# Weighted values of attention for two query tiles at a time, in one row on TensorE

## The chip, the cores and the metric

The kernel runs on one core of a Trainium2 chip. The metric is the device time of one execution in microseconds; of several executions the median is taken.

## What is computed

One layer of an encoder trunk on 1024 positions of width 1024: a SwiGLU feed-forward block, then a mixing block of which one half is attention (8 heads of width 64) and the other a two-directional RWKV-7 scan, then a second feed-forward block, each between RMS norms and added to the residual stream. The change is in the attention:

```python
DILATED_PATTERNS = ((128, 1), (512, 4), (2048, 16))
for window, dilation in DILATED_PATTERNS:
    o, l = _dilated_attention(q, k, v, window, dilation)   # query i sees i + dilation*j, |j| <= window/(2*dilation)
    outs.append(o); lses.append(l)
wts = jax.nn.softmax(jnp.stack(lses, axis=0), axis=0)
o = jnp.sum(wts[..., None] * jnp.stack(outs, axis=0), axis=0)
```

with softmax weights `p = exp(s - m)` within each pattern and values `p @ v / sum(p)`.

## The kernel before

The kernel is written in stages: first feed-forward block (to about 680 us), projections, attention (some 910 to 1180 us), the scan (to about 1530 us), the second feed-forward block. Its author's code states what each step does and in which order it is wanted; a scheduler then places the instructions on each engine's queue, by the order of the code and by what it takes to be ready. An engine works through its queue in that order and waits where data or a buffer are missing. So code that is moved by one step can shift instructions of other steps too.

**Attention.** The first two patterns are handled together in `near` (L694), the third in `far` (L648); `attention` (L766) runs the heads one after the other and lets the far part of the next head run between the steps of the present one. Beside each head but the last, `beside(h)` issues a projection of the RWKV half (`project_rwkv`, L505, tile `zr`, L523): 48 matmuls of 128x512 that depend on nothing in the head, and that the scheduler uses as filling.

`near` works on 8 tiles of 128 queries. A tile sees the keys of up to five blocks of 128: 3, 4, 5, 5, 5, 5, 4 and 3 of them. For each tile t:

- `scores(t)`, L705: queries against keys on TensorE into PSUM (tile `s`, L713 and L714, in two halves of up to 512 and 128 columns; the inputs are in fp32r), then the bias and the row minimum on VectorE (L715, tile `nm`), then the exponential on ScalarE (L718, tile `sb`, with the row sum).
- `turn(t)`, L720: 3 to 5 transposes of 128x128 on TensorE into PSUM (tile `pt`, L727), copied to SBUF by ScalarE or VectorE (L728, tile `e12`; the profile calls it `e`). The pool of this tile has two buffers.
- `values(t)`, L730: for each key block two products, one for each half of the queries, into the PSUM tile `po` (L734, against `vn`). The two halves go to different column halves of TensorE's array (`c` = 0 and 64), so the two products of a block run side by side there. A product of fp32 data shows as two records in the profile; a tile with five key blocks has 10 products and 20 records.

The steps are staggered: `scores(step)`, `turn(step - 1)`, `values(step - 2)`, so that values are asked for in each of the steps 2 to 9, one tile at a time. After the last step VectorE scales `po` (L758, tile `ya`); `po` has one buffer, so the next head's first value product waits for L758.

In `far`, 16 products of 64x65 (L673) go into two PSUM tiles, `po3s` and `po3t`, in turns; one reads the upper half of the array's rows and the other the lower.

Of the kernel before, what the change touches and what calls it, by code (L numbers as in the profile page):

```python
# [10 lines left out]
F32 = mybir.dt.float32  # L11
# [20 lines left out]
def _ap(src, off, pat):  # L32
    return bass.AP(tensor=src.tensor, offset=src.offset + off, ap=pat)
# [130 lines left out]
class _Kernel:  # L164
# [138 lines left out]
    def product(self, psum, x, hl, which):  # L303

        return self.product_into([psum.tile([128, 512], F32, name="gu", tag="gu") for _ in which], x,
                                 [(h[:, k, :], l[:, k, :]) for h, l in hl for k in range(4)], which)
# [387 lines left out]
    def near(self, psum, p, h, sq, kh, kl, v, far, between):  # L694

        nc, V, A, G, T = self.nc, self.nc.vector, self.nc.scalar, self.nc.gpsimd, self.nc.tensor
        hs = slice(h % 2 * 64, h % 2 * 64 + 64)
        nm, d = (p.tile([128, NT], F32, name=n, tag=n) for n in ("nm", "dn"))
        M = p.tile([128, 4 * NT], F32, name="M", tag="M")[:, :NT]
        cc = p.tile([128, 2, NT], F32, name="cc", tag="cc")  # L700
        po = psum.tile([128, NT, 64], F32, name="po", tag="o", bufs=1)
        S_, E_ = {}, {}
        keys = lambda t: (max(0, t - 2), min(NT, t + 3))

        def scores(t):  # L705
            k0, k1 = keys(t)
            n, qs = (k1 - k0) * 128, slice(t * 128, (t + 1) * 128)
            bias = self.bias12[:, (k0 - t + 2) * 128:(k0 - t + 2) * 128 + n]
            s = S_[t] = p.tile([128, 640], F32, name="sb", tag="sb")
            for c in range(0, n, 512):  # L710
                e = min(n, c + 512)
                ps = psum.tile([128, 512], F32, name="s12", tag="s", bufs=2)
                T.matmul(ps[:, :e - c], sq[:, qs], kh[:, k0 * 128 + c:k0 * 128 + e], start=True, stop=False)  # L713
                T.matmul(ps[:, :e - c], sq[:, qs], kl[:, k0 * 128 + c:k0 * 128 + e], start=False, stop=True)  # L714
                V.tensor_tensor_reduce(out=s[:, c:e], in0=ps[:, :e - c], in1=bias[:, c:e], scale=-1.0,  # L715
                                       scalar=nm[:, t:t + 1] if c else 3e38, op0=OP.add, op1=OP.min,
                                       accum_out=nm[:, t:t + 1])
            A.activation(s[:, :n], s[:, :n], AF.Exp, bias=nm[:, t:t + 1], scale=-1.0, accum_out=d[:, t:t + 1])  # L718

        def turn(t):  # L720
            n, s = (keys(t)[1] - keys(t)[0]) * 128, S_.pop(t)
            et = E_[t] = p.tile([128, 640], F32, name="e12", tag="e12")
            for c in range(0, n, 512):
                w = min(n - c, 512)
                pt = psum.tile([128, 512], F32, name="pt12", tag="t", bufs=2)
                for i in range(w // 128):
                    T.transpose(pt[:, i * 128:(i + 1) * 128], s[:, c + i * 128:c + (i + 1) * 128], self.ident)  # L727
                (V.tensor_copy if (t % 2 and not c) else A.copy)(et[:, c:c + w], pt[:, :w])  # L728

        def values(t):  # L730
            (k0, k1), et = keys(t), E_.pop(t)
            for i in range(k1 - k0):
                for c in range(0, 128, 64):
                    T.matmul(po[c:c + 64, t, :], et[:, i * 128 + c:i * 128 + c + 64], v[:, k0 + i, hs], start=(i == 0),  # L734
                             stop=(i == k1 - k0 - 1))

        for step in range(NT + 2):
            if step < NT:
                between(step)
                scores(step)  # L740
            if 1 <= step < NT + 1:
                turn(step - 1)
            if step >= 2:
                values(step - 2)
        f = far
        o = h % 2 * 64
        fd, fm, c12, c3 = f[:, :, o], f[:, :, 65], cc[:, 0], cc[:, 1]
        V.scalar_tensor_tensor(M, fm, -1.0, nm, op0=OP.mult, op1=OP.min)
        V.tensor_tensor(c12, M, nm, op=OP.subtract)
        V.tensor_tensor(c3, fm, M, op=OP.add)  # L750
        A.activation(cc, cc, AF.Exp)
        V.tensor_tensor(d, d, c12, op=OP.mult)
        V.tensor_tensor(M, fd, c3, op=OP.mult)
        V.tensor_tensor(d, d, M, op=OP.add)
        V.reciprocal(d, d)
        V.tensor_tensor(cc, cc, d[:, None, :].to_broadcast([128, 2, NT]), op=OP.mult)
        y = p.tile([128, NT, 64], F32, name="ya", tag="ya", bufs=1)
        V.tensor_tensor(y, po, c12[:, :, None].to_broadcast([128, NT, 64]), op=OP.mult)  # L758
        f3 = f[:, :, 1 - h % 2:65 - h % 2]
        G.tensor_tensor(f3, f3, c3[:, :, None].to_broadcast([128, NT, 64]), op=OP.mult)  # L760
        G.tensor_tensor(y, y, f3, op=OP.add)
        G.tensor_tensor(f3, y, y, op=OP.mult)
        V.tensor_reduce(out=self.ss_a[:, :, h], in_=f3, op=OP.add, axis=AX.X)
        self.nc.scalar.dma_start(_ap(self.ya_d, h * 64, [[512, 128], [128 * 512, NT], [1, 64]]), y)

    def attention(self, psum, p, beside):  # L766
# [34 lines left out]
        for h in range(H):  # L801
# [12 lines left out]
            self.near(psum, p, h, *ST.pop(h), X[h // 2][2], F.pop(h), between)  # L814
            beside(h)


    def prep(self, n, p, psum, big):

# [106 lines left out]
    def values(self, t, ch):  # L926

        for par in range(2):
            o = 64 - par * 64
            self.nc.gpsimd.dma_start(t[o:o + 64, :, par].rearrange("p d a c -> p d (a c)"),  # L930
                                     _ap(self.vt_d, (ch * C * 2 + par) * 256, [[512, 64], [S * 512, 2], [1, 256]]))
# [543 lines left out]
```

## Time and profile before

| | us |
|---|---|
| median of three executions | 2297.95 (2295.15 to 2307.57) |
| span of the profiled execution | 2299.0 |
| TensorE busy in it | 2198.8 (96%) |
| VectorE busy | 1767.3 (77%) |
| ScalarE busy | 1023.6 (45%) |
| attention stage, 920 to 1180: TensorE busy | 254.41 of 260 |

The share of busy time tells which engine is worth reading first; it does not tell whether the engine's time is well used. A matmul is shown as busy from its start to a modelled end, and neighbours overlap in the array, so the cost of a matmul in its place is read from its start to the start of the next. In the timeline a row can stand for several records of one kind in a row ("x12"); its start and the start of the row below it then give what the whole group took.

### The profile page before, as it was taken

The numbers are of one execution on the slowest core, as the hardware profiler recorded it, in microseconds if no ns is written. First come the engines' busy times: TensorE is split into PE (matmuls) and PEld (weight loads), VectorE is DVE, ScalarE is ACT, GpSimd is POOL, SyncE is SP. The second block draws the span as 40 slices with busy tenths as digits, with TensorE's granted clock in tenths as the row PEclk, the third lists the DMA queues.
The fourth block names the chain that finished last, engine by engine and source line by source line (L and its number), as shares of the span: only waits on it lengthen the run. The fifth ranks groups of instructions, "written<-read, shape, count | busy, mean of one in ns | idle before, by whom it ended". The sixth has DMA issues, their size and how long they took to land. (4 is left out here: it accounts for less than half of the span.)

```text
span 2299.0 us, 41391 instructions
## 1 busy us (share of the span) xinstructions
PE 2198.8 (96%) x15556; PEld 1781.8 (77%) x15556; DVE 1767.3 (77%) x2893; ACT 1023.6 (45%) x1925; POOL 537.0 (23%) x673
## 2 busy tenths in 40 slices
PE   7999999999999998999998899999799999999998
PEld 5788888878877676777776777776678888888887
DVE  7999999865676254677679678747999999997566
ACT  5322323354567411666654644455442323335453
POOL 2354443410000011222221111122024444441000
PEclk9999999999999999999999799999899999999999
DMA  5354545486662513654467746357445454548665
GB/s 151 124 183 151 170 147 173 164 266 193 193 225 78 212 72 105 186 147 144 131 178 184 211 136 167 107 173 257 155 135 174 150 174 151 170 152 282 194 194 187
DMA packets 346700, 387.74 MB, mean 169 GB/s; under 512 B 73474, under 2 KB 249346, under 8 KB 346500
## 3 DMA queue, kind: packets, MB, share of 16 engines
q1 hardware_dynamic: 294928, 271.71, 39.2%
q0 software_dynamic: 31216, 100.73, 11.6%
q10 hardware_dynamic: 20356, 12.66, 1.8%
q8 instruction: 122, 2.00, 0.4%
q14 instruction: 78, 0.64, 0.1%
HBM read 258.06 MB, written 126.94 MB: 167 GB/s over the span
## 5 line engine op out<-in xcount | busy, mean ns | idle before, releaser
L81 PE MATMUL gu<-xh,wh 128*128 128x512 f32 x704 | 277.3, 394 | 4.6 <-ACT wh L186 4.5
L186 ACT ACTIVATE wh<-raw 128x512 fp32r<-128x512 f32 (+1 forms) x273 | 168.3, 627 | 252.3 <-PE gu L81 95.7
L81 PE MATMUL gu<-xl,wh 128*128 128x512 f32 x704 | 276.0, 392 | 0.0
L81 PE MATMUL gu<-xh,wl 128*128 128x512 f32 x704 | 275.9, 392 | 0.0
L187 DVE TENSOR_TENSOR wl<-raw,wh 128x512 fp32r<-128x512 f32 (+1 forms) x273 | 270.4, 994 | 3.7 <-ACT wh L186 3.0
L421 PE MATMUL pd<-gl,gwh 128*128 128x512 f32 x616 | 240.6, 391 | 2.6 <-DVE gl L187 2.6
L421 PE MATMUL pd<-gh,gwh 128*128 128x512 f32 x616 | 239.8, 390 | 0.6 <-DVE row L86 0.6
L421 PE MATMUL pd<-gh,gwl 128*128 128x512 f32 x616 | 240.1, 390 | 0.2 <-DVE gwl L187 0.2
L86 DVE TENSOR_TENSOR row<-gu,row 128x512 f32<-128x512 f32 x308 | 206.6, 683 | 25.8 <-PE gu L81 23.5
L187 DVE TENSOR_TENSOR gwl<-graw,gwh 128x512 fp32r<-128x512 f32 (+2 forms) x187 | 118.8, 643 | 124.0 <-ACT gwh L186 122.3
L116 POOL DMA_DIRECT2D d_hid<-row x154 | 84.7, 551 | 546.0 <-DVE row L114 524.2
L186 ACT ACTIVATE gwh<-graw 128x512 fp32r<-128x512 f32 (+2 forms) x187 | 103.1, 554 | 187.2 <-PE pd L421 151.3
L81 PEld LDWEIGHTS gu<-xh,wh 128*128 128x128 f32 x704 | 133.4, 190 | 33.6 <-ACT wh L186 5.6
L81 PEld LDWEIGHTS gu<-xh,wl 128*128 128x128 f32 x704 | 133.2, 189 | 27.7 <-DVE wl L187 0.2
L81 PEld LDWEIGHTS gu<-xl,wh 128*128 128x128 f32 x704 | 133.3, 189 | 27.4
L421 PEld LDWEIGHTS pd<-gl,gwh 128*128 128x128 f32 x616 | 115.7, 188 | 27.8 <-DVE gl L187 3.9
L421 PEld LDWEIGHTS pd<-gh,gwh 128*128 128x128 f32 x616 | 115.6, 188 | 25.5 <-DVE row L86 1.0
L421 PEld LDWEIGHTS pd<-gh,gwl 128*128 128x128 f32 x616 | 115.7, 188 | 24.1 <-DVE gwl L187 0.6
L187 DVE TENSOR_TENSOR gl<-raw,gh 128x512 fp32r<-128x512 f32 x160 | 114.7, 728 | 22.9 <-ACT gh L186 22.6
L94 ACT ACTIVATE row<-row 128x512 f32<-128x512 f32 x44 | 27.8, 633 | 212.0 <-DVE row L86 212.0
L145 POOL TENSOR_TENSOR ws<-ws 128x512 f32<-128x512 f32 x88 | 114.6, 1303 | 1.2
L186 ACT ACTIVATE gh<-raw 128x512 fp32r<-128x512 f32 x160 | 98.1, 622 | 35.5 <-DMA raw<-in_ffn_w_down_dram 22.8
(364 smaller groups left out, 5238.2 us busy)
## 6 DMA issues: line engine op xcount, KB each, us to landing
d_hid<-row POOLq DMA_DIRECT2D x154, 256.0 KB, 2.5
graw<-d_hid SPq DMA_DIRECT2D x132, 256.0 KB, 2.9
raw<-in_ffn_w_gate_dram SPq DMA_DIRECT2D x88, 256.0 KB, 3.1
raw<-in_ffn_w_up_dram SPq DMA_DIRECT2D x88, 256.0 KB, 3.6
ws<-in_ffn_w_down_dram SPq DMA_DIRECT2D x88, 256.0 KB, 4.1
d_ws<-ws POOLq DMA_DIRECT2D x88, 256.0 KB, 2.3
raw<-d_ws SPq DMA_DIRECT2D x88, 256.0 KB, 2.8
raw<-in_ffn_w_down_dram SPq DMA_DIRECT2D x66, 256.0 KB, 3.6
```

The lines of the kernel that those rows point to most:

```text
L81: self.K.nc.tensor.matmul(ps, a[:, k, :], b[:, k, :], start=(k == 0 and i == 0), stop=(k == 3 and i == 2))
L86: add = lambda o, x: V.tensor_tensor(o, ps, x, op=OP.add)
L94: A.activation(y[:, 0], y[:, 0], AF.Silu)
L116: put = lambda n, y: G.dma_start(self.hid[n - 1, j // 2], y)
L145: G.tensor_tensor(o, a, b, op=OP.subtract)
L186: self.nc.scalar.activation(h, src, AF.Copy)
L187: (eng or self.nc.vector).tensor_tensor(l, src, h, op=OP.subtract)
L421: T.matmul(ps[x], a[:, ts], b, start=(m == 0 and k == 0), stop=(m == NM - 1 and k == 2))
```

## The change

`values` takes several tiles and is called at every second step, 3, 5, 7 and 9, with two tiles (the later one first); within a call each product is issued behind the one before it in TensorE's queue (`issue_after`), so that a product of the call can't overtake another. The tile `e12` gets four buffers for two. Arithmetic and the number of instructions are the same.

```diff
-            et = E_[t] = p.tile([128, 640], F32, name="e12", tag="e12")
+            et = E_[t] = p.tile([128, 640], F32, name="e12", tag="e12", bufs=4)
...
-        def values(t):
-            (k0, k1), et = keys(t), E_.pop(t)
-            for i in range(k1 - k0):
-                for c in range(0, 128, 64):
-                    T.matmul(po[c:c + 64, t, :], et[:, i * 128 + c:i * 128 + c + 64], v[:, k0 + i, hs], start=(i == 0),
-                             stop=(i == k1 - k0 - 1))
+        def values(*tiles):
+            last = None
+            for t in tiles:
+                (k0, k1), et = keys(t), E_.pop(t)
+                for i in range(k1 - k0):
+                    for c in range(0, 128, 64):
+                        last = self.in_turn(lambda: T.matmul(
+                            po[c:c + 64, t, :], et[:, i * 128 + c:i * 128 + c + 64], v[:, k0 + i, hs], start=(i == 0),
+                            stop=(i == k1 - k0 - 1)), last)
...
-            if step >= 2:
-                values(step - 2)
+            if step >= 3 and step % 2:
+                values(step - 2, step - 3)
...
+    def in_turn(self, product, last):
+        if last is None:
+            return product().ins
+        with self.tc.issue_after(last):
+            return product().ins
```

What it moves is seen in the order of the instructions on TensorE. The names are those of above, with buffer numbers; L734 before is L736 after. Over the whole stage the 544 products of values form 74 uninterrupted groups before and 43 after, and the form in which the array is used (128x128, 128x64 for values, 64x64 for the far part) changes 181 times before and 124 times after.

TensorE, third head, its first two tiles (exponentials `e_8734` and `e_8750`). Before, the first tile's values stand among projection matmuls:

```order
L523 MATMUL zr<-xl_5415,zh 128x512
L734 MATMUL po<-vn,e_8734 64x64 x6
L523 MATMUL zr<-xh_5414,zl 128x512
```

and the second tile's a good way further down, between transposes and scores:

```order
L727 MATMUL pt_8787<-ident,sb 128x128
L734 MATMUL po<-vn,e_8750 64x64 x8
L713 MATMUL s_8806<-kh,sq 128x512
```

After, both stand there:

```order
L727 MATMUL pt_8781<-ident,sb 128x128
L736 MATMUL po<-vn,e_8750 64x64 x8
L736 MATMUL po<-vn,e_8734 64x64 x6
L713 MATMUL s_8806<-kh,sq 128x512
```

The first tile's group has moved behind the second's, and the projection matmuls around its old place have closed up.

TensorE, the same head, near its end (tiles 4 to 6). Before:

```order
L727 MATMUL pt_8902<-ident,sb 128x128
L734 MATMUL po<-vn,e_8869 64x64 x10
L523 MATMUL zr<-xh_5416,zh 128x512
L727 MATMUL pt_8922<-ident,sb 128x128 x4
L734 MATMUL po<-vn,e_8895 64x64 x10
L523 MATMUL zr<-xl_5417,zh 128x512
```

After:

```order
L523 MATMUL zr<-xh_5416,zh 128x512
L736 MATMUL po<-vn,e_8895 64x64 x2
L727 MATMUL pt_8912<-ident,sb 128x128 x4
L736 MATMUL po<-vn,e_8895 64x64 x8
L736 MATMUL po<-vn,e_8859 64x64 x10
L727 MATMUL pt_8939<-ident,sb 128x128 x3
```

The two tiles' 20 products stand in a row but for four transposes that are let in behind the first two.

TensorE, the same head, the far part of the fourth head (`po3s` and `po3t`). Before, the two tiles' products come in turns, from here on eleven times more:

```order
L734 MATMUL po<-vn,e_8780 64x64 x10
L673 MATMUL po3t<-v_8302,e_8763 64x65 x2
L673 MATMUL po3s<-v_8302,e_8763 64x65
L673 MATMUL po3t<-v_8302,e_8763 64x65
```

After, each tile's eight stand together, with scores between:

```order
L727 MATMUL pt_8822<-ident,sb 128x128
L673 MATMUL po3s<-v_8302,e_8757 64x65 x8
L713 MATMUL s_8850<-kh,sq 128x512
L714 MATMUL s_8850<-kl,sq 128x512
L673 MATMUL po3t<-v_8302,e_8757 64x65 x8
L713 MATMUL s_8854<-kh,sq 128x128
```

What was alternating has become two blocks. Before, the far products of the heads 1, 2, 4, 6 and 8 come in turns, after only those of head 1.

## Rows read from the trace of the kernel before

**Rows 1.** The page: span, and TensorE's busy time in it.
```profile
span 2299.0 us, 41391 instructions
...
PE 2198.8 (96%) x15556; PEld 1781.8 (77%) x15556; DVE 1767.3 (77%) x2893; ACT 1023.6 (45%) x1925; POOL 537.0 (23%) x673
```

**Rows 2.** Two stretches: length; busy PE, PEld, DVE, ACT, POOL; granted clock; DMA share, GB/s.
```profile
920.00:1180.00 260.00, 254.41 (x2527) 203.12 (x2527) 186.97 (x459) 167.51 (x386) 66.70 (x71) 0.99 0.50 150
...
1250.00:1530.00 280.00, 254.15 (x5010) 213.06 (x5012) 195.60 (x570) 139.58 (x247) 50.07 (x87) 0.87 0.59 167
```

**Rows 3.** Waits from 920 to 1180 us: total us, times, longest.
```profile
PEld po L734 <- issue: 8.1, 40, 0.4
...
PEld s L713 <- DVE nm L715: 4.7, 9, 1.3
...
PEld pt L727 <- ACT sb L718: 2.9, 6, 0.8
...
PE s L713 <- DVE nm L715: 2.2, 3, 1.0
...
PE pt L727 <- ACT sb L718: 1.8, 3, 0.7
```

**Rows 4.** Timeline of TensorE around a group of six products: start us, us, instruction.
```profile
989.86 0.40 PE L523 MATMUL zr<-xl,zh 128*128 128x512 f32 x1
990.19 0.57 PE L734 MATMUL po<-vn,e 128*64 128x64 f32 x12
990.68 0.50 PE L523 MATMUL zr<-xh,zl 128*128 128x512 f32 x1
991.02 0.40 PE L523 MATMUL zr<-xh,zh 128*128 128x512 f32 x1
991.26 0.39 PE L523 MATMUL zr<-xl,zh 128*128 128x512 f32 x1
```

**Rows 5.** Timeline: transposes ahead of projection matmuls, and ahead of values.
```profile
971.07 0.71 PE L727 MATMUL pt<-ident,sb 128*128 128x128 f32 x5
971.53 0.49 PE L523 MATMUL zr<-xh,zl 128*128 128x512 f32 x1
971.86 0.39 PE L523 MATMUL zr<-xh,zh 128*128 128x512 f32 x1
...
1004.32 0.73 PE L727 MATMUL pt<-ident,sb 128*128 128x128 f32 x5
1004.98 0.80 PE L734 MATMUL po<-vn,e 128*64 128x64 f32 x20
1005.71 0.50 PE L713 MATMUL s<-kh,sq 128*128 128x512 f32 x1
1006.05 0.39 PE L714 MATMUL s<-kl,sq 128*128 128x512 f32 x1
```

**Rows 6.** Timeline: far products in turns (936.21), and in two blocks (972.18).
```profile
936.21 0.27 PE L673 MATMUL po3s<-v,e 64*64 64x65 f32 x1
...
937.12 0.50 PE L713 MATMUL s<-kh,sq 128*128 128x512 f32 x1
...
972.18 0.96 PE L673 MATMUL po3t<-v,e 64*64 64x65 f32 x16
973.07 0.50 PE L523 MATMUL zr<-xl,zh 128*128 128x512 f32 x1
973.50 0.97 PE L673 MATMUL po3s<-v,e 64*64 64x65 f32 x16
974.40 0.45 PE L734 MATMUL po<-vn,e 128*64 128x64 f32 x6
```

**Rows 7.** Timeline: TensorE's idle time at the start of the third head.
```profile
994.48 0.50 PE L713 MATMUL s<-kh,sq 128*128 128x512 f32 x1 [0.78 <-DVE nm L715]
...
995.34 0.28 PE L714 MATMUL s<-kl,sq 128*128 128x128 f32 x1
...
997.77 0.80 PE L727 MATMUL pt<-ident,sb 128*128 128x128 f32 x5 [0.58 <-ACT sb L718]
```

## The prediction

> **What bounds the kernel now.** I read the page's totals first, then the stretch that the change touches, then single instructions. On the page TensorE is busy for 2198.8 of 2299.0 us [rows 1], so for most of the program the end is set by how fast TensorE gets through its queue. The attention stage is no exception: between 920 and 1180 us TensorE is busy for 254.41 of 260 us, VectorE for 186.97 and ScalarE for 167.51 [rows 2]. The granted clock there is 0.99, so nothing is to be had from the clock. What TensorE waits for in that stretch is little: the waits of matmuls and weight loads for the row minima (L715) come to 4.7 and 2.2 us, those for the exponentials (L718) to 2.9 and 1.8 us [rows 3], and they overlap each other in part. The reader should see that a stage with 98% busy can still hold waste: a matmul counts as busy while it waits for its turn in the array, so the gaps have to be read from start to start, not from the idle column.
>
> One row gives the waste away. The weight loads of the weighted values (`po`) sat idle 40 times, 8.1 us together, and the releaser is "issue": no other engine held them up [rows 3]. Something in TensorE itself costs about 0.2 us where such a group begins.
>
> **What a group of weighted values costs beside its products.** A group of 6 products (12 records) stands between two runs of projection matmuls [rows 4]. In a run these start 0.23 us apart (991.02 to 991.26 is 0.24). Into the group it takes 0.33 (989.86 to 990.19): 0.10 too much. The group takes 0.49 (990.19 to 990.68). A group of 10 products takes 0.73 (1004.98 to 1005.71 [rows 5]), so a product is (0.73 - 0.49)/4 = 0.06 us, and 0.13 of either group is no product. Out of the group the first projection matmul takes 0.34 before the next starts: 0.10 too much. Sum 0.33 us for each group, however long it is.
>
> The same by the other neighbourhood, transposes ahead and scores behind: five transposes take 0.46 us ahead of an fp32r matmul and 0.66 ahead of a group [rows 5], 0.20 too much; the group's own 0.13; behind it 0.34 from one scores matmul to the next, but it is 0.33 behind transposes as well [rows 5], so nothing. Sum 0.33 again. I take 0.33.
>
> **The change part by part.**
>
> 1. Two tiles at a time. By the order in which the products stand, the 544 products form 74 uninterrupted groups before and 43 after, not 32: in 11 places something is still put between (the second place of the order shows one, e_8895 cut in 2 and 8). 31 groups fewer at 0.33 us are **10.2 us** off TensorE's queue.
>
> 2. What the scheduler moves with it. The distant pattern's products (L673) read two halves of the array's rows. Where they alternate between `po3s` and `po3t`, all 16 take 0.91 us (936.21 to 937.12); where the 8 of one stand apart from the 8 of the other, each 8 take as long, 0.89 and 0.90, and the matmul between them 0.43 instead of 0.23 [rows 6]. Alternation is worth 0.89 + 0.43 + 0.90 - 0.91 - 0.23 = 1.08 us a head. Before, 5 of the 8 heads alternate; after, only the first, so 4 heads pay (the third place of the order). In two of these four the run was already cut once (2 and 14, 3 and 13), which leaves about 0.7 less to lose. Together **3.6 us** back on the queue. This is the term that the diff alone doesn't tell.
>
> 3. Shared edges. 7 times before, a group of values stood next to such a distant group and shared its edge; 3 times after. 4 edges of 0.1 to 0.2 us: **0.6 us** back. Groups of an odd number of products leave half of the array's columns unused for one product: 18 before, 12 after, 6 times 0.06: 0.3 us off.
>
> 4. The wait at a head's end. The values of tiles 6 and 7 come after the last copy, 14 products for 6: 8 times 0.06 is 0.5 us more before L758 may read `po`. For seven heads projection matmuls fill TensorE's queue meanwhile; at the last one I count it in full: **0.5 us**. The next head's first group comes one step later than before, so its wait for L758 gets shorter, not longer.
>
> 5. Four buffers. Three tiles of exponentials are alive when the pair is issued; two would stall the third transposes' copy. With four, no copy waits for values. The cost is 5 KB a partition and the shift of the tiles behind it in the same pool. I price it at nothing: the first loads into the pool wait for the same last transposes as before, and the scan stage's first loads start after the last reader of the shifted tiles. If that cover failed, it would be a wait at either end of the stage, once, of the size of the longest in rows 3, 1.3 us.
>
> 6. No DMA is added; SyncE's and GpSimd's queues keep their instructions, a few loads change places with their neighbours.
>
> Sum: -10.2 + 3.6 + 0.6 - 0.3 + 0.5 = **-5.8 us**, on a queue that is the bound for 98% of the stage. Behind it the stage hands on what it gains: the scan starts from its results, and no transfer there is tied to an absolute time. But the scheduler also reorders the scan stage (280 us from 1250 on, TensorE busy for 254.15 [rows 2]). The same products stand there with the same alternations and about as many group edges, so I take 0 for it, with 5 us to either side: a fifth of the 26 us that TensorE is idle there.
>
> [...]
>
> **The rivals.**
>
> *Edges are free.* If weight loads are fetched early enough at a group's edge, the 0.33 us is only how the records are drawn, the 31 edges are worth nothing and the apart halves alone are left: 2298 + 3.6 + 0.5 = 2302 us. Against it stands the 8.1 us in 40 waits of the `po` weight loads with no releaser [rows 3], and that the matmul behind is late as well. [...] Chance 0.08.
>
> *The whole gain, and shorter waits.* Were the waits of TensorE in this stage mostly gone as well (2.2 + 1.8 us by the matmuls' rows [rows 3]) and did the scan's new order save 4 us, -5.8 - 4 - 4 would give 2284 us. For it: the pair of tiles needs data that are a whole step old. Against: the waits sit where a head begins and no projection matmuls are left to fill (994.48 and 997.77 [rows 7]), and there the order keeps the same neighbours. Chance 0.22.
>
> *A new wait: transposes too close behind their scores.* A group that no longer stands between a tile's scores and its transposes takes 0.5 to 0.7 us of cover from the minimum and the exponential. The transposes at 997.77 turn the scores whose last matmul started at 995.34; 0.58 of these 2.43 us TensorE is idle [rows 7]. So the queue's work between the two has to be about 2.4 us, and below that there is a wait. By the order, with the rows' durations, 35 of the 64 tiles lose 0.3 us or more of that work; were all of them to wait, at 0.5 us each, 17.5 us would come on top: 2297.95 - 5.8 + 17.5 = 2310 us, slower by 0.5%. But by the same sum the tiles below 2.4 us are 13 before and 12 after; those that lose cover fall from 3 to 4 us to 2.6 or more. Chance 0.08.
>
> *The chain holds nothing together* (74 groups remain): excluded by the order.
>
> **How the numbers follow.** The profiled execution has a span of 2299.0 us; the median of the three runs, 2297.95, is 1 us below it, so I take nothing for what lies around it and go by the median: 2297.95 - 5.8 = **2292 us**. My forecast (a small gain, within 0.5%) has 0.62. About 0.5%, 11.5 us, is what a measurement of this kernel can tell from no change. Unknowns: the price of an edge 0.30 to 0.36 (1 us either way), the distant halves 3 to 5 us, the waits -4 to +6, the scan order -5 to +5. Added as independent they are about 7 us either way around 2292; reaching to the second rival on one side and past the first on the other gives 2282 to 2304. Below 2286.5 lie most of the second rival and a little of the forecast's edge: faster 0.24. Slower takes most of the third: 0.08. The rest is within 0.5%: 0.68.
>
> **What would show it.** In the profile after, the attention stage from its first far products to the last `po` should be 5 to 7 us shorter; the `po` weight loads' "issue" waits should fall from 40 to about 25 with some 0.2 us each; single groups of 20, 28 or 40 records should show the same 0.13 us beside their products; `po3s` and `po3t` should stand apart at 0.89 us each in all heads but the first. A stage as long as before, with longer waits of transposes for L718, would make the third rival right; a shorter stage and a longer scan would put the error in the scan's new order.

## The result, and the profile after

The changed kernel takes 2309.18 us (median of ten runs, 2302.80 to 2315.24), the kernel before, timed beside it, 2299.28 (ten runs, 2293.64 to 2307.57). The ratio is 1.0040, with a 95% interval of 1.0025 to 1.0055: slower by some 9 us. I had forecast 2292 us, 6 us faster, and 2304 us as the upper end. The interval is 0.3% wide, so the 0.5% that I had taken as what a measurement of this kernel can tell was too coarse.

The first two fences are the page and the two stretches of the profile after, to be set against [rows 1] and [rows 2]; the columns are those of these groups.

```profile
span 2303.7 us, 41396 instructions
...
PE 2193.1 (95%) x15556; PEld 1780.3 (77%) x15556; DVE 1770.8 (77%) x2893; ACT 1022.2 (44%) x1925; POOL 536.0 (23%) x673
```

```profile
920.00:1180.00 260.00, 249.78 (x2525) 202.50 (x2525) 188.95 (x459) 166.96 (x386) 65.63 (x71) 0.98 0.50 150
1250.00:1530.00 280.00, 249.74 (x5051) 210.34 (x5052) 196.84 (x574) 138.74 (x246) 50.66 (x88) 0.90 0.59 167
```

TensorE's busy time falls by 5.7 us over the program, by 4.6 us in the attention stretch and by 4.4 us in the scan's stretch, and yet the program is longer: what was taken off TensorE's queue has come back as time in which it waits. The waits of the attention stretch, as in [rows 3] (L736 is the former L734):

```profile
PEld s L713 <- DVE nm L715: 11.7, 14, 1.9
PEld pt L727 <- ACT sb L718: 5.3, 11, 0.7
...
PEld po L736 <- issue: 3.2, 16, 0.5
...
PE s L713 <- DVE nm L715: 7.8, 7, 1.5
PE pt L727 <- ACT sb L718: 2.2, 6, 0.6
```

The waits of `po` with no releaser went from 40 to 16, with 31 groups fewer. But the scores' matmuls now wait 7.8 us for the row minima where they waited 2.2 [rows 3]: `s` has two buffers, and the next scores need one that VectorE's pass for the row minimum (L715) has read. Six of the seven waits stand at the start of heads 3, 5 and 7. This is the third head in the timeline (start us, us, instruction, idle time before it and what ended it), the place of [rows 7]:

```profile
992.81 0.50 PE L713 MATMUL s<-kh,sq 128*128 128x512 f32 x1 [1.50 <-DVE nm L715]
...
995.90 0.50 PE L713 MATMUL s<-kh,sq 128*128 128x512 f32 x1 [1.00 <-DVE nm L715]
...
997.42 0.81 PE L727 MATMUL pt<-ident,sb 128*128 128x128 f32 x5 [0.57 <-ACT sb L718]
```

Where the kernel before waited 0.78 and 0.58 us [rows 7], this one waits 1.50, 1.00 and 0.57. The distant products stand in two blocks, as the order had said; the blocks take what they took in [rows 6]:

```profile
971.53 0.96 PE L673 MATMUL po3t<-v,e 64*64 64x65 f32 x16
972.43 0.50 PE L523 MATMUL zr<-xl,zh 128*128 128x512 f32 x1
972.86 0.96 PE L673 MATMUL po3s<-v,e 64*64 64x65 f32 x16
973.75 0.45 PE L736 MATMUL po<-vn,e 128*64 128x64 f32 x8
```

**The stages of all profiles.** One profile of each kernel says little here, since the ten executions of the kernel before differ by up to 14 us and those of run 12 by 22. The table gives every profile in three stages: A from the first `kl` subtraction (L690) to the last projection product (L523), which holds the whole attention; B from there to the scan's last copy of `uv` (L976); C from there to the last piece of VectorE's opening of the second feed-forward (L349). In brackets is the part of the stage at a granted clock of 0.50; the clock records of the profiles before and after have two levels, 1.00 and 0.50. "Net" is the length less half of the bracket: what would be left if all of that time had been TensorE's and 1.00 twice as fast as 0.50. That is an estimate from the granted clocks; a group of 14 products, in the last section, took 0.97 us at 1.00 and 1.69 at 0.50. In B, where TensorE also waits, no net is given. Runs 1 to 18 are the experiments, in the order of the next section. "Old order" and "new order" are the orders of the kernels before and after outside the attention's own instructions.

| run | values, order | A us (at 0.50), net | B us (at 0.50) | C us (at 0.50), net |
|---|---|---|---|---|
| before | single, old | 333.3 (23.2), 321.7 | 299.6 (71.7) | 110.0 (6.2), 106.9 |
| 1 | single, old | 331.5 (17.1), 323.0 | 296.3 (64.9) | 109.5 (6.1), 106.5 |
| 8 | single, old, far in turn | 331.3 (17.1), 322.8 | 296.0 (64.9) | 113.3 (13.2), 106.7 |
| 14 | single, old, multiply earlier | 332.6 (22.3), 321.4 | 303.3 (78.5) | 113.5 (13.7), 106.6 |
| 3 | single, new | 334.4 (22.2), 323.3 | 298.0 (61.4) | 115.6 (8.9), 111.1 |
| after | pairs, new | 333.7 (26.2), 320.6 | 297.4 (58.0) | 113.6 (12.0), 107.7 |
| 4 | pairs, new | 335.7 (30.7), 320.3 | 300.9 (68.3) | 116.6 (15.4), 108.9 |
| 2 | pairs, old | 330.2 (27.3), 316.5 | 294.1 (54.6) | 113.1 (13.6), 106.3 |
| 5 | pairs, old in A, new behind | 335.0 (36.2), 316.9 | 296.7 (61.4) | 117.6 (16.8), 109.2 |
| 6 | pairs, new in A, old behind | 333.7 (31.6), 317.9 | 292.5 (47.8) | 110.1 (8.3), 105.9 |
| 9 | pairs, new to the finish | 331.5 (22.4), 320.3 | 301.0 (68.3) | 112.5 (12.6), 106.2 |
| 10 | pairs, old to the finish | 332.3 (32.2), 316.2 | 292.0 (58.0) | 116.2 (15.4), 108.5 |
| 13 | pairs, new, multiply later | 336.0 (30.7), 320.6 | 299.1 (78.5) | 116.0 (13.2), 109.4 |
| 17 | pairs, new to the 4th solve | 335.8 (30.7), 320.5 | 300.1 (61.4) | 109.0 (7.0), 105.5 |
| 18 | as 17, multiply later | 332.7 (23.4), 321.0 | 297.8 (61.4) | 109.6 (6.7), 106.3 |
| 7 | pairs, old, far in turn | 327.0 (23.9), 315.1 | 291.2 (51.2) | 111.3 (9.1), 106.8 |
| 12 | pairs from tile 2 on, old, far in turn | 328.7 (25.2), 316.1 | 292.6 (51.2) | 110.0 (6.4), 106.8 |
| 15 | even pairs, old | 328.1 (23.0), 316.6 | 298.8 (64.9) | 111.6 (8.9), 107.1 |
| 11 | even pairs, old, far in turn | 323.4 (19.6), 313.6 | 297.4 (64.9) | 109.1 (7.2), 105.6 |
| 16 | even pairs, own, far in turn | 318.4 (20.5), 308.1 | 300.0 (64.9) | 109.5 (7.1), 106.0 |

Two profiles of the changed kernel (after, run 4) against three with single values in the old order (before, runs 1 and 8), by their means: A 2.7 us longer, B 1.9, C 4.2, what lies behind C 1.7. That is 10 us, and what the medians say too. Net of the clock A is 2.0 us shorter, a third of the gain that I had forecast for it, and most of the loss lies in places that the diff does not touch.

**The clock of all executions.** The mean granted clock of every execution is on record, and with it half of its time at 0.50. The second table has the means over all executions of a run (6 to 12), less those of the kernel before that were timed beside it (23 to 35): the whole difference, the part that is half of the time at 0.50, and the rest. The standard error is 1 to 2 us for the whole, 1.4 to 2.6 for the clock's part and 0.6 to 1.5 for the rest; the columns are rounded one by one.

| run | whole, us | half of the time at 0.50 | rest |
|---|---|---|---|
| 4: the changed kernel | +11.2 | +9.0 | +2.2 |
| 13: the same, multiply later | +11.9 | +13.0 | -1.1 |
| 3: single, new | +11.6 | +5.5 | +6.1 |
| 14: single, old, multiply earlier | +4.7 | +2.1 | +2.7 |
| 2: pairs, old | -2.6 | +2.5 | -5.0 |
| 5: pairs, old in A, new behind | +8.4 | +9.0 | -0.6 |
| 6: pairs, new in A, old behind | +0.1 | +3.5 | -3.4 |
| 9: pairs, new to the finish | +8.4 | +5.1 | +3.2 |
| 10: pairs, old to the finish | +1.3 | +3.2 | -1.9 |
| 17: pairs, new to the 4th solve | +5.2 | +1.7 | +3.5 |
| 18: as 17, multiply later | +2.7 | +2.3 | +0.5 |
| 7: pairs, old, far in turn | -4.0 | +2.1 | -6.1 |
| 12: pairs from tile 2 on, old, far in turn | -6.0 | -2.1 | -3.9 |

So a large part of the changed kernel's loss goes with more time at a granted clock of 0.50: some 136 us of it against 118. The rest column takes off somewhat too much. Among the executions of one kernel a microsecond more of that half goes with 0.7 us more time, which accounts for three quarters of the variance.

### The profile page after: what moved, and what is told of

It reads as the page before. It is cut to its first block, busy times and chain, and to the rows that moved or that the text cites. A ratio compares the mean times of both kernels' runs of the same rounds, so it can differ in the third digit from the quotient of the medians.

```text
span 2303.7 us, 41396 instructions
## 1 busy us (share of the span) xinstructions
PE 2193.1 (95%) x15556; PEld 1780.3 (77%) x15556; DVE 1770.8 (77%) x2893; ACT 1022.2 (44%) x1925; POOL 536.0 (23%) x673
## 4 chain that ended last, share of the span: by engine, by line
PE 39%; DVE 5%; DMA 3%; ACT 2%; issue 2%; SPq 0%; POOL 0%; DVEq 0%; POOLq 0%; ACTq 0%
PE gu L81 18%; PE pd L421 9%; PE po L1090 2%; PE zr L523 1%; PE st L969 1%; PE pw L1090 1%; PE lp L868 1%; DVE Ti L906 1%; DVE ttmp L904 1%; PE y L969 1%; DMA in<-d_rk 1%; DMA f_y<-d_y 1%; PE xu L973 1%; PE bp L876 1%; DVE lm L870 1%
## 5 line engine op out<-in xcount | busy, mean ns | idle before, releaser
L186 ACT ACTIVATE gh<-raw 128x512 fp32r<-128x512 f32 x160 | 98.0, 621 | 35.2 <-DMA raw<-in_ffn_w_down_dram 22.3
```

What stands on the lines that cost most here:

```text
L186: self.nc.scalar.activation(h, src, AF.Copy)
```

## The experiments

The scheduler orders each engine's instructions by when it thinks them ready. The diff moves the values, and with them the scheduler's clock for everything behind. So most runs separate the two: a kernel gets a table with the names of the instructions outside the attention's own functions, in the order in which they are to stand, and each is tied to its predecessor on its engine. The tie is one of issue order; no wait for completion is added. The table's rows say nothing to a reader:

```
         _Kernel(tc, io, out).run()
+        _pin(nc, tc)
...
+_ORDER = {"PE": "...", "DVE": "...", "Activation": "...", "Pool": "...", "SP": "..."}
...
+def _pin(nc, tc):
...
+    by = {i.name: i for i in nc.cur_bb.bb.instructions}
+    for names in _ORDER.values():
+        row = [by["I-" + n] for n in names.split()]
+        for one, nxt in zip(row, row[1:]):
...
+            tc.add_manual_dep(nxt, one.name, mybir.DependencyInfo(
+                mybir.DependencyClass.NoSync, mybir.DependencyReason.DATA), reason="pin")
```

**Runs 1 to 4: attention or order?** Run 1 is the kernel before with `bufs=4` for `e12`, nothing else:

```
-            et = E_[t] = p.tile([128, 640], F32, name="e12", tag="e12")
+            et = E_[t] = p.tile([128, 640], F32, name="e12", tag="e12", bufs=4)
```

> The kernel before with four buffers for the exponentials and nothing else; the order of every engine stays that of the kernel before. Every theory expects no change: ratio 1.000 within 0.002, some 2299 us, and the attention stage 267 to 268 us long. If it is slower by 3 us or more, the buffers alone carry part of the loss.

Measured: 2296.41 us, ratio 0.9997 (0.9981 to 1.0014). The buffers cost nothing. The chain of `issue_after` can be left out of the account: written without it, the pairs stand in the same order on every engine.

Run 2 is the changed kernel with the old order pinned:

> The changed kernel, but everything outside the attention's own instructions (projections beside it, the scan, the loads) is put on each engine in the order of the kernel before. Theory A, the loss comes from the order that the scheduler gives the scan: the time falls back to that of the kernel before, 2296 to 2301 us, ratio 0.999 to 1.001, and from the last values of the attention to the end of the scan the trace is that of before within 1 us. Theory B, the pairs leave TensorE idle at the heads' starts and the lower granted clock or a shifted transfer costs the rest: it stays at 2306 to 2310 us, ratio 1.003 to 1.005.

Measured: 2296.91 us, ratio 0.9990 (0.9974 to 1.0007). Run 3 is the opposite, the kernel before with the new order pinned:

> The kernel before, values one tile at a time, but everything outside the attention in the order of the changed kernel. Theory A: as slow as the changed kernel, 2305 to 2310 us, ratio 1.003 to 1.005, with the attention stage as long as before (267 to 268 us) and the scan 3 to 8 us longer. Theory B: as before, 2297 to 2301 us, ratio 0.999 to 1.001.

Measured: 2310.12 us, ratio 1.0046 (1.0029 to 1.0062), although it computes its values one tile at a time. The two runs settle the first question: the loss goes with the order, not with the pairs. Theory A's sign in the stages is missing in both profiles: B of run 2 is 2 to 6 us shorter than in the kernel before, at less time at 0.50, and B of run 3 is no longer than there (298.0 against 296.0 to 299.6). Run 4 is the changed kernel once more:

> The changed kernel once more, for a second profile beside the three others on one chip: ratio 1.003 to 1.006. What differs between its trace and the first one of the same kernel is not the change: if the attention ends within 1 us of the first profile and the end of the scan differs by 3 us or more, the spread of runs arises behind the attention.

Measured: 2308.84 us, ratio 1.0038 (1.0021 to 1.0055). Its stage A is 2.0 us longer than in the first profile, with 4.5 us more at 0.50 (net 320.3 against 320.6), and B is 3.5 us longer: the spread of runs arises in both.

**Runs 5 and 6: order beside the attention, or behind it?** Both are the changed kernel with a mixed table; the cut is the last instruction of the attention on each engine.

> The changed kernel; outside the attention's own instructions the order is that of the kernel before up to the last attention instruction of each engine, and that of the changed kernel behind it. Theory A1, the loss sits in the new order behind the attention: ratio 1.002 to 1.005, 2302 to 2309 us, and the first wait of the transposes of the decays' block for the vector engine, over 3 us near 1281 us, is there again. Theory A2, the loss sits in the new order of the projections beside the attention: ratio 0.999 to 1.001, 2296 to 2300 us.

Measured: 2306.74 us, 1.0035 (1.0018 to 1.0052): A1. The transposes' wait is there, but 1.65 us long and at 1283.5 us, after one of 2.33 us by the block's products ahead of it.

> The reverse: the changed kernel with its own order beside the attention and the order of the kernel before behind it. Theory A1: ratio 0.999 to 1.002, 2296 to 2302 us, the waits for the running maximum at the start of heads 3, 5 and 7 still 1.5 and 1.0 us. Theory A2: ratio 1.003 to 1.005, 2305 to 2309 us.

Measured: 2298.66 us, 1.0004 (0.9993 to 1.0016): A1 again. One detail was missed: the waits at the heads' starts did not stay, the scores wait for the minima 2.6 us in all (3 times), since with the projections' order fixed the scheduler sets the attention's own instructions between them in another way.

**Runs 7 and 8: the distant products.** Both have the old order; the products of a head are chained, in the pairs' kernel (7) and in the kernel before (8):

```
+        last = None
         for r in range(16):
             c, g, j = r // 8, r % 8 // 2, r % 2
-            T.matmul(po[j][row(c), g, :], e[row(j), g, row(c)], v3[row(j), c * 4 + g, vs], start=True, stop=True)
+            last = self.in_turn(lambda: T.matmul(
+                po[j][row(c), g, :], e[row(j), g, row(c)], v3[row(j), c * 4 + g, vs], start=True, stop=True), last)
```

> Pairs, everything outside the attention in the order of the kernel before, and the sixteen far products of a head chained so that they alternate between the two row halves. In the second experiment's kernel six of the eight heads had them in two blocks of eight; a block pair cost some 0.9 us more in the trace of before. If that term of my sum is right: 4 to 6 us faster than the second experiment's kernel, ratio 0.996 to 0.998, 2289 to 2293 us. If blocks cost nothing beside other work: as that kernel, ratio 0.999 to 1.000.

Measured: 2293.78 us, 0.9987 (0.9975 to 0.9999), 3 us below run 2.

> The kernel before with nothing but the far products chained to alternate in every head, the rest in its old order. Three of eight heads had them in blocks. The far term right: 2 to 3 us faster, ratio 0.9985 to 0.9992; wrong: 1.000. Beside the seventh run it gives the price of pairs alone, with equal far products: theory edges-pay says the seventh is 5 to 7 us faster than this one, theory waits-take-it-back says within 2 us.

Measured: 2298.21 us, 1.0002 (0.9989 to 1.0016): no gain. In stage A, net, the chain is worth 1.4 us with pairs (run 2 against 7, six heads had blocks) and nothing with single values (runs 1 and 8, three heads). At 1.4 us for six heads that is 0.2 us a head, where I had 0.9; runs 11 and 15 below show more. With the far products in turn on both sides, pairs make A 7.7 us shorter (315.1 against 322.8, net), with 43 groups of values for 74: about a quarter of a microsecond for a group. Runs 7 and 8 differ by 4.4 us, between what the two theories had said.

**Runs 9 and 10: the scan, or its finish?**

> The changed kernel; everything outside the attention in the changed kernel's order up to the scan's finish (the first yc product on TensorE, and what stands ahead of the same place on the other engines), behind it in the order of the kernel before. By the stages of the runs so far the new order costs 1 us beside the attention, 3 us from the last projection to the last xu product, 3 us from there to the last output product and 2 us up to the second feed-forward's first sums. Theory F, the finish carries most: ratio 1.0005 to 1.0015, 2299 to 2301 us. Theory S, the scan carries most: ratio 1.0025 to 1.004, 2304 to 2307 us. By the stages: 1.002, 2302 us.

Measured: 2305.76 us, 1.0037 (1.0022 to 1.0053).

> The reverse: the order of the kernel before up to the finish, the changed kernel's behind it. Theory F: ratio 1.002 to 1.004, 2302 to 2307 us, and 20.2 us instead of 18.4 from the last output product to the last piece of the second feed-forward's opening. Theory S: ratio 0.999 to 1.001, 2296 to 2300 us. By the stages: 1.002, 2302 us.

Measured: 2300.88 us, 1.0005 (0.9987 to 1.0024). The scan carries most, theory S: in the second table the new order of the scan costs 8 us (run 9 against 6), that of the finish 4 (run 10 against 2). The finish's part is seen in the stages: in C the profiles with the new finish have a net of 107.7 to 111.1, those with the old one 105.5 to 107.1. That is 2 to 3 us which run 10's interval still admits. What the stages had said for both runs, 1.002, came out for neither.

**Runs 13 and 14: one instruction.** What does the scan's new order hold that costs time? The timeline of run 3 shows it, 30 us behind the last projection. VectorE masks the four parts of a decay block (`lm`, L860) so that their PSUM buffers come free; the transposes into `bp` (L866) need these buffers. First VectorE in run 1, with the old order, then VectorE and TensorE in run 3, with the new:

```profile
1271.03 1.29 DVE L860 TENSOR_TENSOR lm<-lp,k_tri 128x512 f32<-128x512 f32 x2 [0.27 <-PE lp L858]
1272.73 0.69 DVE L860 TENSOR_TENSOR lm<-lp,k_tri 128x512 f32<-128x512 f32 x1 [0.42 <-PE lp L858]
1273.88 0.69 DVE L860 TENSOR_TENSOR lm<-lp,k_tri 128x512 f32<-128x512 f32 x1 [0.46 <-PE lp L858]
1278.25 0.69 DVE L1088 TENSOR_TENSOR yat<-yat,rs 128x512 f32<-128x512 f32 x1 [3.67 <-DMA yat<-d_ya]
```

```profile
1274.29 1.28 DVE L860 TENSOR_TENSOR lm<-lp,k_tri 128x512 f32<-128x512 f32 x2
1279.53 0.69 DVE L1088 TENSOR_TENSOR yat<-yat,rs 128x512 f32<-128x512 f32 x1 [3.96 <-DMA yat<-d_ya]
1280.14 1.28 DVE L860 TENSOR_TENSOR lm<-lp,k_tri 128x512 f32<-128x512 f32 x2
```

```profile
1277.20 0.43 PE L911 MATMUL pa<-ident,X 32*32 32x32 f32 x14
1280.88 1.11 PE L866 MATMUL bp<-ident,bk 64*128 64x64 f32 x8 [3.25 <-DVE lm L860]
```

In both kernels the multiply of `yat` (L1088) waits almost 4 us for its load. In the old order it does so behind the four masks, where nobody needs VectorE. In the new order it stands between the second and the third, the two masks wait behind it, and TensorE waits for them. Run 13 is the changed kernel in its own order with this one instruction moved back, run 14 the kernel before with it moved up:

```
 (run 13, VectorE)                           (run 14, VectorE)
-L870 TENSOR_TENSOR lm<-lp,k_tri x2          -L860 TENSOR_TENSOR lm<-lp,k_tri x4
+L870 TENSOR_TENSOR lm<-lp,k_tri x4          +L860 TENSOR_TENSOR lm<-lp,k_tri x2
 L1098 TENSOR_TENSOR yat<-yat,rs              L1088 TENSOR_TENSOR yat<-yat,rs
-L870 TENSOR_TENSOR lm<-lp,k_tri x2          +L860 TENSOR_TENSOR lm<-lp,k_tri x2
```

> The changed kernel with one instruction of the vector engine moved: in the scan's first step the multiply of yat, which waits some 4 us for its load, stands behind all four mask multiplies of the decays' block instead of between the second and the third; every other instruction as in the changed kernel. Theory Q, the masks held in the vector engine's queue behind that load are the price of the new scan: the transposes' wait of 3.2 to 3.9 us near 1278 us is gone, the time falls by 2 to 4 us, ratio to the kernel before 1.002 to 1.003. Theory R, the new order costs a little at many places and later waits take the gap over: within 1 us of the changed kernel, ratio 1.0035 to 1.005.

Measured: 2310.17 us, 1.0058 (1.0035 to 1.0081). The wait is gone, as theory Q has it, and the time is not: a miss. The second table says where the gain is: the rest is 3.3 us less than in run 4, and half of the time at 0.50 is 4.0 us more (six executions).

> The kernel before with the same multiply moved two places up, between the second and the third mask multiply, and nothing else. Theory Q: 2 to 4 us slower than before, ratio 1.001 to 1.002, with a new wait of TensorE's transposes of some 3 us near 1280 us. Theory R: ratio 1.000 within 0.0005.

Measured: 2303.13 us, 1.0024 (1.0007 to 1.0041), with a wait that is longer than I had thought:

```profile
1283.74 1.11 PE L866 MATMUL bp<-ident,bk 64*128 64x64 f32 x10 [5.45 <-DVE lm L860]
```

One moved instruction makes the kernel before slower, by 3.5 us in the medians and 5.5 by the ratio. Taking it out of the changed kernel gave nothing that the times show.

**Runs 17 and 18: the same, with nothing behind that could take the gain over.** In run 17 the new order ends with the fourth solve of the scan; run 18 moves the multiply there.

> The changed kernel; outside the attention its own order only up to the fourth solve of the scan (some 116 us behind the last projection), from there the order of the kernel before. By the stages, 4 to 5 us of the loss sit there and 1 us beside the attention, less the 1 us that pairs give in the old order: ratio 1.001 to 1.0025, 2300 to 2304 us, with the transposes' wait of 3 to 4 us near 1279 us. If the later steps carry the loss: 0.999 to 1.0005.

Measured: 2304.38 us, 1.0018 (1.0001 to 1.0036), as the stages had said.

> The seventeenth run's kernel with the multiply of yat behind the four masks, as in the thirteenth. Theory Q: the transposes' wait is gone and the time is 2 to 4 us below the seventeenth, ratio 0.9995 to 1.001. Theory R, later waits take it over: within 1 us of the seventeenth.

Measured: 2302.47 us, 1.0014 (0.9995 to 1.0032). The stretch from the last projection to the fourth solve, in run 17 and in run 18 (columns as in [rows 2]):

```profile
1249.46:1368.50 119.04, 100.19 (x1875) 84.17 (x1874) 88.93 (x251) 63.87 (x109) 18.76 (x35) 0.81 0.69 185
```

```profile
1244.58:1359.70 115.12, 100.43 (x1875) 84.30 (x1874) 89.25 (x250) 63.91 (x109) 18.79 (x35) 0.82 0.70 192
```

With the move the stretch is 3.9 us shorter, at the same busy time of TensorE and nearly the same clock. The medians are only 1.9 us apart, and their intervals overlap, so the times alone do not prove it, and the traces are one of each. But three pairs of kernels differ in this one instruction, and in the rest column all three agree: 3.3 us (run 13 against 4), 2.7 (14 against the kernel before) and 3.0 (18 against 17), each with an error of 1.2 to 1.8. So the place of the multiply costs some 3 us (2.1 to 3.2 with only 0.7 of the clock's part taken off). In run 13 the time at 0.50 hides it; why there is more of it in that run is not shown.

**Runs 11, 12, 15, 16: is there a version that keeps the gain?** The waits at the heads' starts come up where the first tile's values no longer stand ahead of the scores. Run 11 issues the pairs at the even steps, so that tile 0 goes alone at step 2; far products chained and old order as in run 7:

```
-            if step >= 3 and step % 2:
-                values(step - 2, step - 3)
+            if step in (2, NT + 1):
+                values(step - 2)
+            elif step >= 3 and step % 2 == 0:
+                values(step - 2, step - 3)
```

> Order outside the attention and far products as in the seventh run; the pairs are issued at the even steps, so that the first tile's values go alone at step 2 and stand ahead of the scores that wait at a head's start. 39 groups of value products instead of 43. Theory edges-pay: 1 to 3 us below the seventh run, ratio 0.997 to 0.9985, 2290 to 2293 us. Theory clock, what the waits and the groups give is taken back by more stretches at the lower level: as the seventh, 0.9985 to 0.9995.

Measured: 2286.82 us, 0.9954 (0.9935 to 0.9973): below both kernels, and 3 to 6 us below what I had expected of it. It is not the cover that I had meant: in the attention stretch its scores wait 4.0 us for the minima, run 7's 3.1. Run 12 leaves the pairs at the odd steps and issues tiles 0 and 1 alone:

```
-            if step >= 3 and step % 2:
+            if step in (2, 3):
+                values(step - 2)
+            elif step >= 3 and step % 2:
                 values(step - 2, step - 3)
```

> As the seventh run, but the first two tiles' values go alone, at steps 2 and 3, and the pairs begin with tiles 2 and 3: 51 groups instead of 43, cover for the waits at the heads' starts back. Eight more groups at 0.33 us cost 2.6 us; if the waits of heads 3, 5 and 7 fall by what the seventh has more than the kernel before, 1 to 3 us come back. Edges-pay expects 0 to 2 us above the seventh, ratio 0.9985 to 0.9995; a theory in which the waits alone decide expects 1 to 3 us below it, 0.997 to 0.9985.

Measured: 2289.77 us, 0.9963 (0.9943 to 0.9983): 4 us below run 7 in spite of eight groups more; the theory in which the waits alone decide had 1 to 3. But its scores wait 3.0 us for the minima in the attention stretch and its transposes 1.6 for the exponentials, run 7's 3.1 and 1.7, and in A the net is 316.1 against 315.1. The second table tells what these 4 us are: run 12's rest is 2.2 us above run 7's, about as the theory that edges pay has it, and half of its time at 0.50 is 4.2 us less. So it is no sign for the waits.

> As the eleventh run (pairs at the even steps, everything outside in the old order), but the far products left to the scheduler, in two blocks of eight in three of the heads. If the even steps are what pays: ratio 0.996 to 0.9975, 2289 to 2292 us, 2 to 4 us above the eleventh. If the far products are what pays: as the second run, 0.999 to 1.0005.

Measured: 2295.05 us, 0.9993 (0.9974 to 1.0011). Even steps alone give little; with the far products in turn they give 3 us net in A (316.6 against 313.6). The two runs also differ in the groups of values, 43 against 39, so the far products of the three heads are not all of it.

> As the eleventh run, but with no order given from outside: the scheduler sets it. It moves 330 of TensorE's instructions outside the attention against the kernel before (the changed kernel 673). If any reordering of the scan costs: ratio 0.998 to 1.001. If it costs only where it makes TensorE wait: as the eleventh, 0.9945 to 0.9965.

Measured: 2286.89 us, 0.9963 (0.9946 to 0.9980), with no table at all. This is a version that beats both kernels as plain code: even pairs, four buffers, far products in turn, the order left to the scheduler. Its stage A, beside that of the changed kernel (first row):

```profile
912.44:1246.12 333.68, 315.20 (x2927) 255.21 (x2928) 248.52 (x615) 198.99 (x450) 74.82 (x90) 0.96 0.54 159
```

```profile
912.29:1230.66 318.37, 305.90 (x2928) 247.24 (x2928) 245.93 (x618) 198.32 (x449) 73.15 (x88) 0.97 0.57 168
```

The same number of products, 9.3 us less busy time and 6.0 us less idle time. That it also has a reordered scan and is not slower shows that a new order is not bad as such.

## Why the prediction was wrong

**The sum for the attention came out right by luck, and for another program.** I had -5.8 us for the changed kernel. It is pairs in the old order that show it: there, and net of the clock, stage A has 321.7, 323.0 and 322.8 us with single values and 316.5, 316.9 and 316.2 with pairs (runs 2, 5 and 10): 6.0 us less. But two terms were too large and nearly cancel: with the far products in turn on both sides 31 groups are worth 7.7 us (runs 8 and 7), where step 1 had 10.2, and step 2's 3.6 us for the distant products are mostly not seen. That edges of groups cost time is borne out, at about a quarter of a microsecond each and not 0.33, and the `po` waits with no releaser fell as step 1 had said, further than I thought (16, not 25).

**The term for the distant products** (3.6 us) was too large. Put back in turn, six heads give 1.4 us (runs 2 and 7) and three heads 0.2 (runs 1 and 8), with the groups of values unchanged. With the pairs at even steps three heads and four groups fewer give 3.0 us (runs 15 and 11), so the price of a head stays open between 0.1 and 1 us. The block of 8 takes its 0.89 us as in [rows 6], but the timeline's arithmetic counted the whole difference as TensorE's loss.

**The order beside the attention** was not in the sum. It takes 4 us back: with pairs and the new order A is 320.3 to 321.0 us, net (run 6, where the attention's own instructions stand in another way, 317.9). The rows for it are the scores' waits at heads 3, 5 and 7, 7.8 us where the old order with the same pairs has 1.6 (run 6 2.6). Here is run 2's attention stretch, to be read against the fence of the profile after:

```profile
PEld s L713 <- DVE nm L715: 4.9, 15, 0.8
PEld po L736 <- issue: 4.1, 19, 0.5
...
PE s L713 <- DVE nm L715: 1.6, 4, 0.6
```

This is near my third rival (a stage as long as before, with a new wait), but not its mechanism. I had looked for transposes too close behind their scores, and those waits grew from 1.8 to 2.2 us only [rows 3]. What is late is a step further up: at a head's start the projection products had been used up ahead of the scores, and the group of values that had stood there had gone one step down. This is read from the order; no run changes it by itself.

**The clock** was not in the sum either. I had said that nothing is to be had from it. In A the kernels with single values spend 17 to 23 us at a granted clock of 0.50, those with pairs at the odd steps 22 to 36 (26.2 and 30.7 in the two profiles of the changed kernel). Their means are 8 us apart, which is 4 us of TensorE's time: most of what the pairs save in run 2, whose time is that of the kernel before. Over all executions of run 2 it is 2.5 us of 5.0, with an error of 1.8.

**The scan's order was the step that failed.** I wrote: the same products stand there with the same alternations and about as many edges, so I take 0, with 5 us to either side. Run 3 has nothing but the new order and loses 12 us; behind the attention alone it is 11 us (second table, run 5 against 2 and run 4 against 6), where I had 0. Some 5 us of these are the rest and some 6 half of the time at 0.50. Counting TensorE's edges prices what TensorE does, not what it waits for, and in the scan it waits. Two such waits were found. On VectorE an instruction that waits for a DMA had come in front of two that free PSUM, which costs some 3 us. At the finish TensorE waits 1.5 to 2.0 us for the load of `f_sg` in all six profiles with the new finish, and at most 0.2 in the others. The step went by TensorE's order in this stage and left VectorE's and the loads' out. And its bound of 5 us was a fifth of the idle time, which a reordering does not respect: it can add idle time as well as take it.

Of the four buffers (nothing, run 1) the prediction was right; the wait at a head's end was not looked at by itself.

**What stays open.** Run 13's times show none of the multiply's gain; its profile has 78.5 us at 0.50 in B, as much as run 14's and more than any other. Why the new order goes with more time at 0.50, which is about half of what it costs, was not found; the records of the unprofiled executions do not tell in which stage it lies. The wait for `f_sg` was seen and not taken out by a run. And why A is 7 us shorter, net, in run 16 than in run 7 has not been taken apart.

## What to carry to other kernels

Where a scheduler sets the order, price the whole program that comes out of a diff: pin the old order around the edit (or the new order around the old code) before believing that the edit is what the time shows. Read the order of the engine that frees buffers, and look for an instruction that waits for a DMA in front of one that TensorE needs; one such place cost some 3 us where 31 groups of values saved 6. Work that is taken out of TensorE's queue at a place where it waits next is not all saved: here 6 us of waits came up at the heads' starts. And set the time at each level of the granted clock beside the times of all executions before a difference of a few microseconds is given a cause.

## What the runs showed of the hardware

In run 4 TensorE's granted clock fell from 1.00 to 0.50 with no single pause above 1.5 us in the 8 us ahead of it. The third head shows three waits in six microseconds, with 5.52 of 8 us busy at 1.00 from 990 to 998, and then 3.4 us at 0.50 while TensorE is busy all the time:

```profile
990.00:998.00 8.00, 5.52 (x28) 3.98 (x27) 6.73 (x13) 2.03 (x5) 4.12 (x4) 1.00 0.74 218
999.20:1002.60 3.40, 3.40 (x35) 2.86 (x34) 0.65 (x5) 3.40 (x9) 0.00 (x0) 0.50 0.61 189
```

```profile
994.41 0.50 PE L713 MATMUL s<-kh,sq 128*128 128x512 f32 x1 [1.50 <-DVE nm L715]
...
997.48 0.50 PE L713 MATMUL s<-kh,sq 128*128 128x512 f32 x1 [0.98 <-DVE nm L715]
...
999.00 1.19 PE L727 MATMUL pt<-ident,sb 128*128 128x128 f32 x5 [0.58 <-ACT sb L718]
1000.12 1.76 PE L736 MATMUL po<-vn,e 128*64 128x64 f32 x28
1001.81 0.80 PE L713 MATMUL s<-kh,sq 128*128 128x512 f32 x1
```

The same waits in the first profile of the same kernel (1.50, 1.00 and 0.57 us) were not followed by a fall at that place, the granted clock being 1.00 from 922 to 1129 us, so one profile does not tell what a wait costs. There, at a granted clock of 1.00, the 14 products of values took 0.97 us from their start to the next matmul, where they take 1.69 at 0.50 in run 4:

```profile
998.15 1.04 PE L736 MATMUL po<-vn,e 128*64 128x64 f32 x28
999.12 0.50 PE L713 MATMUL s<-kh,sq 128*128 128x512 f32 x1
```

So waits of 1.50, 0.98 and 0.58 us stand ahead of the fall in one profile; that they brought it about is not shown, since the same waits in the other had no fall behind them.

The time at 0.50 and the length go together in B too: in the profiles with little of it (47.8 to 54.6 us, runs 2, 6, 7 and 12) B is 5 to 8 us shorter than in the kernel before (71.7), with the same order and the same products. Which of the two brings the other about is not shown. Much of the spread between executions of one kernel, up to 22 us, goes with the granted clock: half of the time at 0.50 accounts for three quarters of its variance, as said below the second table.
